# A two-layer decoder trunk on one core: tensors laid out on the host, no transposes, GpSimd silent in the recurrent part, another order of blocks

## The chip, the cores and the metric

The kernel runs on one core of a Trainium2 chip. A core has five engines that run their own instruction queues in order: TensorE (PE, matrix multiplies into PSUM; its weight loads are listed as PEld), VectorE (DVE), ScalarE (ACT), GpSimd (POOL) and SyncE (SP, which here only issues DMA transfers). They work on SBUF, an on-chip memory of 128 partitions, and wait for each other through semaphores. The metric is the device time of one execution in microseconds.

## The reference, cut to what matters

There are 1024 tokens of 1024 channels, and two layers. Layer 0 mixes tokens by a gated linear recurrence (RG-LRU), layer 1 by stick-breaking attention; each is followed by a dense SwiGLU network of width 2816, and a last RMS norm ends it.

```python
def rms_norm(x, g):
    return x * lax.rsqrt(jnp.mean(x * x, axis=-1, keepdims=True) + 1e-6) * g

def rg_lru_block(x, ...):
    u = x @ w_in + b_in                      # (1024 x 1024) @ (1024 x 2048)
    gate_branch, rec = u[..., :1024], u[..., 1024:]
    rec = causal_depthwise_conv(rec, conv_w, conv_b)          # 4 taps
    r, i = sigmoid(rec_blocks @ gate_w + gate_b)              # 4 diagonal blocks of 256
    log_a = -8 * r * softplus(-lam);  a = exp(log_a)
    h[t] = a[t] * h[t-1] + sqrt(-expm1(2 * log_a)) * (i * rec)[t]
    return (gelu(gate_branch) * h) @ w_out + b_out

for layer in range(2):
    h = h + mixer(rms_norm(h, mix_norm[layer]))
    h = h + swiglu_ffn(rms_norm(h, ffn_norm[layer]))
return rms_norm(h, final_norm)
```

All is fp32. The kernel keeps that precision by splitting each operand of a product into a high part (rounded to the fast fp32r type) and a low part (the difference), and by adding three products.

## The kernel before, in words

**Tiles.** Activations are kept with channels on the partitions: 8 channel tiles (ND) of 128, each as two halves (NH) of 512 tokens (NB). A product of a weight tile with a half is `mm3` (L141 to L143): three matmuls of 512 columns, high by high, high by low, low by high. A projection of one column of 128 output channels over both halves is 2 x 8 x 3 = 48 matmuls.

**First phase (L251 to L361).** x comes in token order, so TensorE transposes it (L301, 64 blocks of 128x128 against the identity). ScalarE writes the high part `xh` with the norm's gain (L304), VectorE the low part `xl` (L309), and a plain copy `hc` goes back to device memory as `hd` (16 stores), which is later loaded as the residual h. ScalarE takes the squares of the rows with a running sum (L314); from them come `rcol`, the 1/rms factors of the tokens, and `rbc`, the same factors spread over the partitions by small matmuls (L189). The norm's gains, biases and other vectors come in nine small loads as rows and are turned by one more transpose (L345). Beside this, the first two columns of the recurrent branch, A0 and A1, are projected. In this phase the order on every engine is written by hand.

**Recurrent block.** Blocks of work are named by a letter and an index, and their order is one string in the code:

```python
"A0 A1 B0 A2 G0 A3 Y0 B1 Y1 A4 G1 A5 B2 Y2 A6 G2 A7 B3 Y3 B4 Y4 G3 B5 Y5 B6 Y6"
```

A is a column of the recurrent branch: projection, scaling by `rbc` (`u`, L444), the four-tap convolution (`rec`, ScalarE L446 and three VectorE operations L448), and its split into `rh` (L450) and `rl` (L451). G is a pair of tiles: the two gates by matmuls over both tiles' `rh` and `rl`, then sigmoid, tanh, exp and square root on ScalarE (L472 to L480), seven elementwise operations and the recurrence itself on VectorE as one scan (L475 to L483). B is a column of the gate branch with its gelu (`gb`, L490, L491), Y the product of gelu and scan (L495). `last_tile` does B7 and splits the results for the output projection (`ob_ps`). By hand only TensorE's order is fixed here; a scheduler places the others' instructions by its own costs. The weights of a column are one load of 512 KB; ScalarE rounds the high part `whi` (L120), GpSimd subtracts for the low part `wlo` (L124), into a ring of three pairs of tiles. Products go to four PSUM tiles in turn (`ptile`).

**Middle.** The output projection, the first feed-forward network, attention (about 950 to 1500 us) and the second feed-forward network follow. The networks use a scheme of seven products in place of eight for each 2x2 arrangement of blocks; `ORDER` is the order of the seven, `Weights` loads and combines their weights, and `VISITS` lists the passes over the output. After each finished output tile `squares` adds its square to `acc`, on ScalarE (L211) and GpSimd (L212).

**End.** `finish` computes the last products of output tiles 0 and 4 (`last`, L1212 to L1225), the row statistics (`stats`), and in `turn` transposes the result back to token order (L1236, 64 blocks), scales it by `rcol` on ScalarE or VectorE (L1238, L1240) and stores it (L1241).

Of the kernel before, what the change touches and what calls it, by code (L numbers as in the profile page):

```python
# [29 lines left out]
V_MIX, V_FFN, V_FIN, V_BIN, V_CW, V_CB, V_GB, V_LAM, V_BO = 0, 16, 32, 40, 56, 88, 96, 112, 120  # L30


@with_exitstack
def trunk(
# [3 lines left out]
    mix_norm,  # L38
    ffn_norm,
    final_norm,  # L40
    lru_w_in,
    lru_b_in,
    lru_conv_w,
    lru_conv_b,
    lru_gate_w,
    lru_gate_b,
    lru_lambda,
    lru_w_out,
    lru_b_out,
# [5 lines left out]
    stage=None,  # L55
# [55 lines left out]
    def load_raw(src, shape):  # L111
        raw = rp.tile([P, D], F32, tag="raw", name="raw")
        view = raw if len(shape) == 1 else raw.rearrange("p (a b) -> p a b", a=shape[0])
        nc.sync.dma_start(view, src)
        return raw

    def split(raw, pool=None, tag="w", bufs=None, lo_eng=None, parts=1):
        pool = pool or wpool[0]
        hi = pool.tile([P, D], F32R, tag=tag, name="whi", bufs=bufs)
        nc.scalar.copy(hi, raw)  # L120
        lo = pool.tile([P, D], F32R, tag=tag, name="wlo", bufs=bufs)
        for i in range(parts):
            c = slice(i * D // parts, (i + 1) * D // parts)
            (lo_eng or nc.gpsimd).tensor_sub(lo[:, c], raw[:, c], f32(hi)[:, c])  # L124
        return hi, lo

    def cols(w, c0, n=P):
        return w[:, c0 : c0 + n].rearrange("(k p) c -> p k c", p=P)

    def load_cols(w, c0, **kw):  # L130
        hi, lo = split(load_raw(cols(w, c0), (ND,)), **kw)
        k3 = lambda t: t.rearrange("p (k c) -> p k c", k=ND)
        return k3(hi), k3(lo)

    def load_rows(w, r0, **kw):
        hi, lo = split(load_raw(w[r0 : r0 + P, :].rearrange("p (a b) -> p a b", a=1), (1,)), **kw)
        k3 = lambda t: t.rearrange("p (k c) -> p k c", k=ND)
        return k3(hi), k3(lo)
# [14 lines left out]
    class Mix:  # L153
# [8 lines left out]
        def load(self, i):  # L162
            self.raw[i] = load_raw(cols(self.src, self.order[i] * P), (ND,))
# [21 lines left out]
    def broadcast_r(ps_pool, tag, n):  # L185
        ps = ps_pool.tile([P, NB], F32, tag=tag, name="rb_ps")
        for i in range(4):
# [7 lines left out]
            )  # L195
        nc.vector.tensor_copy(rbc[n], ps)

    def stats(acc, ps_pool, tag, n, i0=0, i1=4):
        ps = ps_pool.tile([P, NB], F32, tag=tag, name="st_ps")
        for i in range(i0, i1):  # L200
# [28 lines left out]
    def open_h(nm):  # L229
# [3 lines left out]
        for j in range(ND // 2):  # L233
            for d in (j, j + ND // 2):
                for n in range(NH):
                    nc.sync.dma_start(h[d][n], hd[d][n])
# [4 lines left out]
    w_in, gw = lru_w_in[0], lru_gate_w[0]  # L241
# [8 lines left out]

    with ExitStack() as st, tc.manual_schedule(engines={E.PE, E.Activation, E.DVE, E.Pool, E.SP}):  # L251
        sp = st.enter_context(tc.tile_pool(name="sp", bufs=1))
        sps = st.enter_context(tc.tile_pool(name="sps", bufs=4, space=PSUM))
        vraw = sp.tile([P, P], F32, name="vraw")
        vmix = sp.tile([P, P], F32, name="vmix")
        g0 = sp.tile([P, ND], F32, name="g0")
        nc.scalar.dma_start(vmix[0:ND, :], mix_norm[0:1].rearrange("a (b c) -> (a b) c", c=P))
        xt = [sp.tile([P, 4, D], F32, name=f"xt{n}") for n in range(NH)]
        aw = []

        def load_x(n, g):
            cs = slice(g * 2 * P, (g + 1) * 2 * P)
            nc.sync.dma_start(
                xt[n][:, :, cs], x[0, n * NB : (n + 1) * NB, cs].rearrange("(i p) c -> p i c", p=P)
            )

        for g in range(3):
            load_x(0, g)
        aw.append(load_raw(cols(w_in, D), (ND,)))
        load_x(0, 3)  # L270
        aw.append(load_raw(cols(w_in, D + P), (ND,)))
        load_x(1, 0)
        load_x(1, 1)
        for base, src in (
            (V_MIX, mix_norm.rearrange("a (b c) -> (a b) c", c=P)),
            (V_FFN, ffn_norm.rearrange("a (b c) -> (a b) c", c=P)),
            (V_FIN, final_norm.rearrange("(b c) -> b c", c=P)),
            (V_BIN, lru_b_in.rearrange("a (b c) -> (a b) c", c=P)),
            (V_CW, lru_conv_w.rearrange("a k (b c) -> (a k b) c", c=P)),
            (V_CB, lru_conv_b.rearrange("a (b c) -> (a b) c", c=P)),  # L280
            (V_GB, lru_gate_b.rearrange("a g (b c) -> (a g b) c", c=P)),
            (V_LAM, lru_lambda.rearrange("a (b c) -> (a b) c", c=P)),
            (V_BO, lru_b_out.rearrange("a (b c) -> (a b) c", c=P)),
        ):
            nc.sync.dma_start(vraw[base : base + src.shape[0], :], src)
        load_x(1, 2)
        load_x(1, 3)
        ssum = sp.tile([P, NT], F32, name="ssum")
        ms = sp.tile([P, NT], F32, name="ms0")
        junk = sp.tile([P, D], F32, name="junk")  # L290
        pst = lambda name: sps.tile([P, NB], F32, tag="tp", name=name)
        k3 = lambda t: t.rearrange("p (k c) -> p k c", k=ND)

        ps = pst("vps0")
        nc.tensor.transpose(ps[:, 0:ND], vmix[0:ND, :], ident[0:ND, 0:ND])
        nc.vector.tensor_copy(g0, ps[:, 0:ND])

        def group(n, d):
            ps = pst("tp")
            for i in range(4):  # L300
                nc.tensor.transpose(ps[:, i * P : (i + 1) * P], xt[n][:, i, d * P : (d + 1) * P], ident)  # L301
            hc = sp.tile([P, NB], F32, tag="hc", name="hc", bufs=8)
            g = g0[:, d : d + 1]
            nc.scalar.activation(xh[d][n], ps, AF.Copy, scale=g)  # L304
            if d % 4 == 3:
                nc.scalar.copy(hc, ps)
            else:
                nc.vector.tensor_copy(hc, ps)
            nc.vector.scalar_tensor_tensor(xl[d][n], ps, g, f32(xh[d][n]), op0=ALU.mult, op1=ALU.subtract)  # L309
            nc.sync.dma_start(hd[d][n], hc)  # L310

        def square_rows(n, i):
            b = 4 * n + i
            nc.scalar.activation(junk, xt[n][:, i, :], AF.Square, accum_out=ssum[:, b : b + 1])  # L314

        def row_factors(n):
            nn = slice(4 * n, 4 * n + 4)
            nc.vector.tensor_scalar(ms[:, nn], ssum[:, nn], 1.0 / D, EPS, op0=ALU.mult, op1=ALU.add)
            rstd(rcol[:, nn], ms[:, nn])

        def wsplit(i):
            hi, lo = split(aw[i])
            aw[i] = (k3(hi), k3(lo))

        pa = [psl[0].tile([P, S], F32, tag="a", name="a_ps") for _ in range(2)]
        for d in range(6):
            group(0, d)
        wsplit(0)
        for d in (6, 7):
            group(0, d)  # L330
        wsplit(1)
        for i in range(4):
            square_rows(0, i)
# [192 lines left out]

# [1074 lines left out]
```

## Time and profile before

| | us |
|---|---|
| time, median of 3 runs (2211.14 to 2213.21) | 2211.43 |
| span of the profiled execution | 2213.1 |
| its own time | 2213.21 |
| TensorE busy | 2174.9 |
| VectorE busy | 1728.4 |
| ScalarE busy | 1152.4 |
| GpSimd busy | 288.8 |

The profiled execution is the slowest of the three, 1.8 above the median. Times in rows of a timeline are microseconds from the start of the span: start, duration, engine, line, operation, output <- inputs, shapes, count, and in brackets how long the engine had been idle before and what released it. Rows of groups give the count, the total busy time, the mean of one in ns, and the idle time before. Matmuls are pipelined: a row of 0.39 us is followed by the next one's start 0.23 us later. The lines that carry the argument stand in the prediction.

### The profile page before, as it was taken

The page shows a single profiled execution, that of the slowest core. Times are in us where ns is not written, and L with a number is a line of the kernel's source. Part 1 is how long each engine was busy: PE and PEld are TensorE (multiplying, and loading weights), DVE is VectorE, ACT ScalarE, POOL GpSimd, SP SyncE. Part 2 cuts the span into 40 slices and gives each one's busy share as a digit, 9 for nine tenths or more (in the row PEclk, how much of TensorE's full clock was granted, in tenths as well). Part 3 has the DMA queues.
Part 4 walks back from the last instruction along what each step waited for, and adds up shares of the span by engine and source line. Part 5 has one row for each costly group of instructions (what it writes and reads, how often), then busy time and mean ns, then how long its engine had stood idle before and what let it go on. Part 6 is the DMA issues. An engine that isn't in the chain of part 4 may idle for free.

```text
span 2213.1 us, 28506 instructions
## 1 busy us (share of the span) xinstructions
PE 2174.9 (98%) x10120; PEld 1802.8 (81%) x10120; DVE 1728.4 (78%) x2383; ACT 1152.4 (52%) x2031; POOL 288.8 (13%) x379
## 2 busy tenths in 40 slices
PE   8999999999999999999999999989999999999998
PEld 6888888888888888878888887878888888888887
DVE  6887778677777887878888888876876777788876
ACT  5577444444444544656666666653533444454556
POOL 2222020000000000004333333331000000000002
PEclk9999999999999999999999999999999999999999
DMA  7111412334443864453333333532133444467442
GB/s 230 48 48 38 133 39 71 106 124 152 143 157 133 272 194 123 144 144 85 95 89 102 98 88 99 169 137 71 39 110 124 148 147 137 149 233 231 136 148 86
DMA packets 298703, 277.74 MB, mean 125 GB/s; under 512 B 16312, under 2 KB 215104, under 8 KB 298560
## 3 DMA queue, kind: packets, MB, share of 16 engines
q1 hardware_dynamic: 298544, 275.91, 40.0%
q8 instruction: 80, 1.31, 0.2%
q14 instruction: 63, 0.52, 0.1%
q10 hardware_dynamic: 16, 0.00, 0.0%
HBM read 175.71 MB, written 74.97 MB: 113 GB/s over the span
## 4 chain that ended last, share of the span: by engine, by line
PE 84%; DVE 8%; ACT 3%; DMA 2%; issue 1%; SPq 1%; DVEq 0%; ACTq 0%
PE p_ps L143 18%; PE p_ps L141 18%; PE p_ps L142 18%; PE ob_ps L141 2%; PE ob_ps L142 2%; PE ob_ps L143 2%; PE qk_ps L143 2%; PE qk_ps L141 2%; PE qk_ps L142 2%; PE a_ps L143 2%; PE a_ps L142 2%; PE a_ps L141 2%; PE wt_ps L1437 2%; DVE F L1425 2%; PE z_ps L1400 1%
## 5 line engine op out<-in xcount | busy, mean ns | idle before, releaser
L1426 POOL TENSOR_TENSOR w<-w,F 128x128 f32<-128x128 f32 (+1 forms) x192 | 185.2, 965 | 315.0 <-DVE F L1423 177.6
L143 PE MATMUL p_ps<-vh,wcl 128*128 128x512 f32 x524 | 204.2, 390 | 0.5 <-DVE wcl L682 0.5
L143 PE MATMUL p_ps<-vh,wbl 128*128 128x512 f32 x524 | 204.3, 390 | 0.3 <-DVE wbl L672 0.2
L143 PE MATMUL p_ps<-vh,wal 128*128 128x512 f32 x524 | 204.1, 389 | 0.1
L141 PE MATMUL p_ps<-vh,wbh 128*128 128x512 f32 x524 | 204.2, 390 | 0.0
L141 PE MATMUL p_ps<-vh,wch 128*128 128x512 f32 x524 | 204.1, 389 | 0.0
L142 PE MATMUL p_ps<-vl,wbh 128*128 128x512 f32 x524 | 203.9, 389 | 0.0
L142 PE MATMUL p_ps<-vl,wch 128*128 128x512 f32 x524 | 203.9, 389 | 0.0
L142 PE MATMUL p_ps<-vl,wah 128*128 128x512 f32 x524 | 203.9, 389 | 0.0
L141 PE MATMUL p_ps<-vh,wah 128*128 128x512 f32 x524 | 203.9, 389 | 0.0
L668 ACT CAST wbh<-sb 128x1024 fp32r<-128x1024 f32 (+2 forms) x69 | 69.6, 1009 | 193.6 <-DVE sb L652 193.6
L212 POOL TENSOR_TENSOR acc<-acc,rbc 128x512 f32<-128x512 f32 x30 | 40.5, 1349 | 773.3 <-ACT rbc L211 773.3
L1423 DVE TENSOR_TENSOR_SCAN F<-F,unit 128x128 f32<-128x128 f32 (+3 forms) x128 | 128.5, 1004 | 4.4 <-ACT F L1419 4.3
L1446 ACT CAST th<-wt_ps 128x512 fp32r<-128x512 f32 x192 | 93.3, 486 | 73.2 <-PE wt_ps L1437 71.2
L1447 DVE TENSOR_TENSOR tl<-wt_ps,th 128x512 fp32r<-128x512 f32 x192 | 104.9, 547 | 29.1 <-ACT th L1446 28.1
L141 PE MATMUL qk_ps<-vh,whi 128*128 128x512 f32 x264 | 118.4, 449 | 0.6 <-ACT vh L215 0.6
L143 PEld LDWEIGHTS p_ps<-vh,wbl 128*128 128x128 f32 x524 | 98.3, 188 | 22.4 <-DVE wbl L672 2.0
L143 PEld LDWEIGHTS p_ps<-vh,wcl 128*128 128x128 f32 x524 | 98.3, 188 | 22.0 <-DVE wcl L682 1.6
L143 PEld LDWEIGHTS p_ps<-vh,wal 128*128 128x128 f32 x524 | 98.3, 188 | 21.4 <-DVE wal L663 1.0
L142 PEld LDWEIGHTS p_ps<-vl,wch 128*128 128x128 f32 x524 | 98.4, 188 | 20.4
L141 PEld LDWEIGHTS p_ps<-vh,wbh 128*128 128x128 f32 x524 | 98.4, 188 | 20.4 <-ACT ta L1053 0.2
L142 PEld LDWEIGHTS p_ps<-vl,wah 128*128 128x128 f32 x524 | 98.3, 188 | 20.4
(400 smaller groups left out, 5837.7 us busy)
## 6 DMA issues: line engine op xcount, KB each, us to landing
raw<-in_ffn_w_in SPq DMA_DIRECT2D x88, 512.0 KB, 3.9
vl<-pd SPq DMA_DIRECT2D x128, 256.0 KB, 3.7
pd<-U SPq DMA_DIRECT2D x90, 256.0 KB, 2.3
raw<-in_ffn_w_out SPq DMA_DIRECT2D x56, 256.0 KB, 3.8
raw<-in_attn_w_qkv SPq DMA_DIRECT2D x24, 512.0 KB, 3.9
raw<-in_lru_w_in SPq DMA_DIRECT2D x16, 512.0 KB, 4.1
acc<-pd SPq DMA_DIRECT2D x28, 256.0 KB, 2.6
pph<-rbc SPq DMA_DIRECT2D x28, 256.0 KB, 2.5
```

Of the source, the lines that this page charges most:

```text
L141: nc.tensor.matmul(ps, lhsT=wh, rhs=mh, start=first, stop=False, **kw)
L142: nc.tensor.matmul(ps, lhsT=wh, rhs=ml, start=False, stop=False, **kw)
L143: nc.tensor.matmul(ps, lhsT=wl, rhs=mh, start=False, stop=last, **kw)
L212: (eng or nc.gpsimd).tensor_add(acc[n], acc[n], sq)
L668: nc.scalar.copy(self.full(self.wb), self.full(self.sb))
L1400: nc.tensor.matmul(ps[:, 0 : c1 - c0], lhsT=lhsT, rhs=KL[q][hx][:, c0:c1], start=False, stop=True)
L1423: nc.vector.tensor_tensor_scan(rev, rev, unit[:, NB - n :][:, ::-1], first, op0=ALU.mult, op1=ALU.add)
L1425: nc.vector.tensor_tensor_scan(rev, rev, rev, first, op0=ALU.mult, op1=ALU.bypass)
L1426: nc.gpsimd.tensor_mul(wt, wt, F[:, 1 : n + 1])
L1437: nc.tensor.transpose(tp[:, c : c + P], W[q, hx, j, kb // 4][:, (kb % 4) * P : (kb % 4 + 1) * P], ident)
L1446: nc.scalar.copy(th[:, q0:], tp[:, q0:])
L1447: nc.vector.tensor_sub(tl[:, q0:], tp[:, q0:], f32(th)[:, q0:])
```

## The change

- The host lays out x as [channel tile, half, 128, 512], the weights as tiles whose partition lines are contiguous, and the vectors as one `table` that is one load, on ScalarE's queue. The result is stored as [channel tile, half, 128, 512] and put in order by the host. All transposes on TensorE are gone, `hc` and `hd`'s first stores too: h is loaded from x.
- The first phase projects four columns, `FIRST` = A0, A1, B0, A2, from `lru_first`, which holds their weights by k. For half 0 the four are interleaved over k, each k as soon as its x tile and weights are there; then half 1 column by column. Squares of x are taken tile by tile on ScalarE, added on VectorE, and summed over partitions by small matmuls (`column_stats`). All four PSUM tiles are taken in this phase.
- In the recurrent block the low parts of weights are subtracted on VectorE rather than GpSimd. The `+ 1.0` on `a` goes from VectorE to ScalarE. The order of the blocks is another.
- In the second network the squares' adds go from GpSimd to VectorE, the last visit's products come in another order, of which 3 and 6 are handed to `finish`, the last weights have tiles of their own (`we`), and the square root's table is loaded early.
- `finish` spreads the factors over the partitions (`factor`) and multiplies each output tile (`give`), on VectorE or, for some tiles, on GpSimd, before storing it; the last stores alternate between the queues of SyncE and ScalarE.

The core of the diff:

```diff
+FIRST = (ND, ND + 1, 0, ND + 2)
...
-            (lo_eng or nc.gpsimd).tensor_sub(lo[:, c], raw[:, c], f32(hi)[:, c])
+            (lo_eng or nc.vector).tensor_sub(lo[:, c], raw[:, c], f32(hi)[:, c])
...
+        for k in range(ND):
+            nc.sync.dma_start(xr[k][0], x[k, 0])
+            nc.sync.dma_start(fr[k].rearrange("p (t c) -> p t c", t=4), lru_first[k])
+        for k in range(ND):
+            nc.sync.dma_start(xr[k][1], x[k, 1])
...
+        bank = half(pa[FIRST[3]], 1)
+        for k in range(ND):
+            nc.scalar.copy(fh[k], fr[k])
+            x_hi(k, 0)
+            x_square(k, 0)
+            nc.vector.tensor_sub(fl[k], fr[k], f32(fh[k]))
+            x_lo(k, 0)
+            if k:
+                x_add(k - 1, 0)
+            for t, j in enumerate(FIRST):
+                c = slice(t * P, (t + 1) * P)
+                mm3(half(pa[j], 0), fh[k][:, c], fl[k][:, c], xh[k][0], xl[k][0], k == 0, k == ND - 1)
+        x_add(ND - 1, 0)
+        for k in range(ND):
+            x_hi(k, 1)
+            x_lo(k, 1)
+        for k in range(3):
+            x_square(k, 1)
...
+        def second(i, ks):
+            for k in ks:
+                c = slice(i * P, (i + 1) * P)
+                mm3(half(pa[FIRST[i]], 1), fh[k][:, c], fl[k][:, c], xh[k][1], xl[k][1], k == 0, k == ND - 1)
+
+        def spread_to(n):
+            spread(bank, n)
+            nc.vector.tensor_copy(rbc[n], bank)
+
+        column_stats(sacc[0], bank, 0)
...
+        second(0, range(4))
+        spread_to(0)
...
+        second(0, range(4, ND))
+        second(1, range(4))
+        column_stats(sacc[1], bank, 1)
+        second(1, range(4, ND))
+        second(2, range(2))
+        spread_to(1)
+        second(2, range(2, ND))
+        second(3, range(ND))
...
-                V.tensor_scalar_add(a, a, 1.0)
+                nc.scalar.activation(a, a, AF.Identity, bias=1.0)
...
-            for what in "A0 A1 B0 A2 G0 A3 Y0 B1 Y1 A4 G1 A5 B2 Y2 A6 G2 A7 B3 Y3 B4 Y4 G3 B5 Y5 B6 Y6".split():
+            for what in "A0 A1 B0 A2 B1 G0 A3 Y0 Y1 A4 B2 G1 A5 Y2 A6 B3 Y3 G2 A7 B4 Y4 G3 B5 Y5 B6 Y6".split():
...
-                    squares(h, d, n, rbc, acc, first=n not in begun_sq)
+                    squares(h, d, n, rbc, acc, V, first=n not in begun_sq)
...
+                rest = [lambda: tail(3, range(3)), lambda js: tail(6, js)]
+                for k, i in enumerate((0, 1, 2, 4, 5) if last_two else ORDER):
...
+        def factor(n, i0, i1):
+            cs = slice(i0 * P, i1 * P)
+            spread(half(ob, n), n, i0, i1)
+            nc.scalar.copy(half(rs, n)[:, cs], half(ob, n)[:, cs])
+
+        def give(n, i0, i1, ds, slow=(), queues=(nc.sync,)):
+            cs = slice(i0 * P, i1 * P)
+            for k, d in enumerate(ds):
+                t = h[d][n][:, cs]
+                if d in slow:
+                    nc.gpsimd.tensor_mul(t, t, half(rs, n)[:, cs])
                 else:
+                    nc.vector.tensor_mul(t, t, half(ob, n)[:, cs])
+                queues[k % len(queues)].dma_start(out[d, n][:, cs], t)
...
+        for x in range(2):
+            last(x, *first)
+        third()
+        sixth(range(0, 1))
+        stats(acc[0], pp, "p", 0)
+        sixth(range(1, 3))
+        last(0, *mid)
+        factor(*first)
+        give(*first, (1, 2, 3, 5), (3,))
+        last(1, *mid)
+        give(*first, (6, 7, 0, 4), (7,))
+        last(0, *end)
+        stats(acc[1], pp, "p", 1, 0, 2)
+        last(1, *end, lambda: factor(*mid), lambda: give(*mid, (1, 3), (3,)))
+        give(*mid, (2, 5))
+        stats(acc[1], pp, "p", 1, 2, 4)
+        give(*mid, (6, 7, 0, 4), (7, 4))
+        factor(*end)
+        give(*end, (1, 2, 3, 5, 6, 0, 7, 4), (3, 7), (nc.sync, nc.scalar))
```

More of the change, by code (lines that the diff above doesn't have):

```diff
@@ L54, in trunk @@
     out,
-    stage=None,
 ):
@@ L162, in load @@
         def load(self, i):
-            self.raw[i] = load_raw(cols(self.src, self.order[i] * P), (ND,))
+            self.raw[i] = load_raw(self.src[self.order[i]])
         def proc(self, i):
@@ L183, in rstd, with spread @@
         nc.vector.tensor_mul(dst, sq, t)
-    def broadcast_r(ps_pool, tag, n):
-        ps = ps_pool.tile([P, NB], F32, tag=tag, name="rb_ps")
-        for i in range(4):
+    def spread(ps, n, i0=0, i1=4):
+        for i in range(i0, i1):
             b = 4 * n + i
@@ L195, in broadcast_r @@
             )
+    def broadcast_r(ps_pool, tag, n):
+        ps = ps_pool.tile([P, NB], F32, tag=tag, name="rb_ps")
+        spread(ps, n)
         nc.vector.tensor_copy(rbc[n], ps)
@@ L286, in trunk @@
[L286 to L325, printed above, removed]
@@ L1191, in mix_out_ffn_in @@
                 nxt = ahead
-                if kind == "v" and not final:
+                if kind == "v" and final:
+                    if x == 2:
+                        open_end()
+                elif kind == "v":
                     if x == 2:
```

311 lines of the change are left out of this document (125 added, 186 removed).

## The prediction

> **What bounds the kernel now.** I read the page first (busy shares, the chain that ended last), then windows of the stages that the change touches, then timelines at the start, between the last two gate stages and at the tail.
>
> ```profile
> PE 2174.9 (98%) x10120; PEld 1802.8 (81%) x10120; DVE 1728.4 (78%) x2383; ACT 1152.4 (52%) x2031; POOL 288.8 (13%) x379
> PE 84%; DVE 8%; ACT 3%; DMA 2%; issue 1%; SPq 1%; DVEq 0%; ACTq 0%
> ```
>
> TensorE is busy for 98% of the span of 2213.1 us, so the change pays only where it removes work of TensorE, its idle time or its cold clock. The windows say where these are (window, length, busy time of PE, PEld, DVE, ACT, POOL, granted clock, DMA share, GB/s):
>
> ```profile
> 0.00:50.00 50.00, 39.25 (x198) 32.28 (x199) 30.91 (x77) 29.52 (x46) 13.19 (x12) 1.00 0.75 244
> 100.00:150.00 50.00, 50.00 (x223) 41.39 (x222) 44.35 (x35) 30.32 (x28) 14.44 (x5) 1.00 0.17 49
> 154.30:198.80 44.50, 44.50 (x197) 36.60 (x195) 38.65 (x30) 29.66 (x27) 11.86 (x4) 1.00 0.17 48
> 2186.30:2207.30 21.00, 17.59 (x141) 16.41 (x139) 14.02 (x38) 13.26 (x24) 0.22 (x1) 1.00 0.40 149
> ```
>
> The start holds 10.75 us of idle TensorE, and the tail 3.4. In the recurrent block TensorE never rests, and VectorE comes next with 44.35 of 50.
>
> **Start.** The first transposes, warm ones later, the projections, and the end of the recurrent stage:
>
> ```profile
> 4.52 4.55 PE L301 MATMUL tp<-ident,xt 128*128 128x128 f32 x20 [1.18 <-DMA xt<-in_x]
> 19.12 1.03 PE L301 MATMUL tp<-ident,xt 128*128 128x128 f32 x8
> L304 ACT ACTIVATE xh<-tp,g 128x512 fp32r<-128x512 f32 x16 | 10.3, 686 | 2.2 <-PE tp L301 2.2
> L309 DVE SCALAR_TENSOR_TENSOR xl<-tp,g,xh 128x512 fp32r<-128x512 f32 x16 | 11.5, 739 | 0.0
> L451 DVE TENSOR_TENSOR rl<-rec,rh 128x1024 fp32r<-128x1024 f32 x8 | 9.8, 1219 | 0.0
> L450 ACT CAST rh<-rec 128x1024 fp32r<-128x1024 f32 x8 | 8.4, 1050 | 26.1 <-DVE rec L448 26.1
> 41.77 1.16 PE rb_ps L189 x8
> 240.26 0.39 PE L141 MATMUL a_ps<-xh,whi 128*128 128x512 f32 x1
> 241.62 0.39 PE L141 MATMUL ob_ps<-xh,whi 128*128 128x512 f32 x1
> ```
>
> Between the last two rows lie six matmuls: 1.36 / 6 = 0.227 us each. The stage has 20 blocks of 48 matmuls (16 projected columns, 4 gate blocks). The changed kernel projects four of them at the start; the other 16 are 768 matmuls, 174.3 us. The kernel before has that much left at 241.6 - 174.3 = 67.3. When does the changed one?
> Its first x tile and first weight slice are 512 KB together, as one x piece was before, so they land near 4.5 us; two ScalarE operations of the 686 ns kind follow, and the first matmul starts at 5.8. Per k TensorE has 12 x 0.227 = 2.7 us; VectorE 3 x 0.7 = 2.1; ScalarE about 2.0; the transfer of 512 KB at the window's 244 GB/s 2.1. So TensorE sets the pace: 96 x 0.227 = 21.8 us. The 20 first transposes took 4.55 us, warm ones 1.03 / 8 = 0.129 each, so a cold start costs 4.55 - 20 x 0.129 = 2.0 us; it was spent on transposes beside waiting and now falls on real matmuls. Half 0 ends at 5.8 + 21.8 + 2.0 = 29.6. Half 1 is 21.8 more; the two spreads are the 1.16 of the rb_ps row, the 8 small statistics matmuls about as much. One wait is new: on VectorE's queue three splits of later weights (L116, 1.22 each) stand ahead of the statistics of half 0, so the row factors come near 34.8 while TensorE wants to spread them at 33.0; I take 1.0 of that 1.8. End of the first phase: 29.6 + 21.8 + 1.2 + 1.2 + 1.0 = 54.8; gain 12.5 us (bounds 9 to 16: all waits doubled, or none and a warm clock). The nine vector loads, the 16 write-backs of h and their copies were off TensorE's path, and SP's queue only gets shorter: nothing.
> The Trainium skill ("TensorE: Matmul & The Clock Gate", Part 1) has the first 3.4 us of activity at half clock, in a window that runs freely; it speaks against the change, which puts projections there. Half of 3.4 is 1.7 us by that estimate, so the rule makes the gain 12.8 and not 12.5.
>
> **Recurrent block.** The stretch between gate stages G2 and G3, with its split operations on GpSimd:
>
> ```profile
> 154.30 0.39 PE L141 MATMUL g_ps<-rh,whi 128*128 128x512 f32 x1
> 162.42 1.28 DVE L448 SCALAR_TENSOR_TENSOR rec<-u,vc,rec 128x1024 f32<-128x1024 f32 x1
> 164.40 1.23 DVE L475 TENSOR_TENSOR gs<-gs,rec 128x1024 f32<-128x1024 f32 x1 [0.69 <-ACT gs L473]
> 167.80 1.22 DVE L477 SCALAR_TENSOR_TENSOR ga<-ga,gt 128x1024 f32<-128x1024 f32 x1 [1.04 <-ACT ga L476]
> 169.06 1.23 DVE L478 SCALAR_TENSOR_TENSOR ga<-ga,gt 128x1024 f32<-128x1024 f32 x1
> 170.32 1.23 DVE L479 SCALAR_TENSOR_TENSOR gt<-ga 128x1024 f32<-128x1024 f32 x1
> 172.59 0.69 DVE L481 TENSOR_SCALAR ga<-ga 128x1024 f32<-128x1024 f32 x1
> 174.64 1.23 DVE L482 TENSOR_TENSOR gs<-gs,gt 128x1024 f32<-128x1024 f32 x1 [1.36 <-ACT gt L480]
> 175.90 2.29 DVE L483 TENSOR_TENSOR_SCAN y<-ga,gs 128x1024 f32<-128x1024 f32 x1
> 178.09 3.46 POOL L124 TENSOR_TENSOR wlo<-raw,whi 128x1024 fp32r<-128x1024 f32 x1 [18.57 <-ACT whi L120]
> 179.34 3.29 DVE L478 SCALAR_TENSOR_TENSOR ga<-ga,gt 128x1024 f32<-128x1024 f32 x1
> 183.16 2.82 DVE L479 SCALAR_TENSOR_TENSOR gt<-ga 128x1024 f32<-128x1024 f32 x1
> 189.23 2.56 POOL L124 TENSOR_TENSOR wlo<-raw,whi 128x1024 fp32r<-128x1024 f32 x1 [4.34 <-ACT whi L120]
> 189.46 4.48 DVE L483 TENSOR_TENSOR_SCAN y<-ga,gs 128x1024 f32<-128x1024 f32 x1
> 198.84 0.50 PE L142 MATMUL g_ps<-rl,whi 128*128 128x512 f32 x1
> ```
>
> Three VectorE operations that met a split of GpSimd took 3.29, 2.82 and 4.48 where their likes took 1.23, 1.23 and 2.29: 5.8 us that go with GpSimd. In return VectorE gets two or three splits of 1.22 per stretch and gives one kind of 0.69 (L481) to ScalarE, which has 20 of 50 us free.
> The Trainium skill ("SBUF — State Buffer", Who interferes with whom) calls the shared port an exclusive lock: a VectorE instruction with two SBUF inputs and a GpSimd one that reads SBUF shut each other out for the whole instruction. The three rows agree; by it the splits cost VectorE more on GpSimd (about 2 us each) than the 1.22 on its own queue.
> What counts is when rl of tile 7 is ready, the last input of G3 (the 198.84 row; before, it came just in time, with A7, B3 and B4 behind G2). The new order moves B3 ahead of G2: from G2's start only G2, A7 and B4 are left, 3 x 48 x 0.227 = 32.7, and rl is needed 0.9 later (fifth matmul), at 33.6. VectorE's queue: it meets G2's first result 164.40 - 154.30 = 10.1 after its start; from there to rl stand, in the new order, 13 operations of 1.22, two scans (4.6), two u and two gb halves of 0.69 (2.8) and three L448 of 1.28 (3.8): 27.1, and the waits for ScalarE of 1.04 and 1.36 stay. 10.1 + 27.1 + 2.4 = 39.6: **G3 stalls 6.0 us** (bounds 0, where rl is pulled ahead to the end of A7 at 21.8 + 9; and 11, with the 5.85 us idle that VectorE has in the window row). G1 and G2 keep four blocks of distance, 43.6, against 38.6 of VectorE's work: no stall up to 5 us idle.
> **G0 stalls 2.6 us:** the order puts B1 ahead of G0, and ScalarE's queue has the high part of A4's weights (a cast like rh, 1.05), which needs the ring slot that B1's last matmul frees, ahead of rh of tile 1 (1.05); rl (1.22) follows; 0.7 is covered by G0's first three matmuls, which need tile 0 alone (0 to 4). Behind that cast on ScalarE wait rh, gb and rec; behind rl on VectorE gb.
>
> **Attention and FFN.** Weights come in whole lines of 4 KB instead of 512 B. The waits that a faster transfer could touch:
>
> ```profile
> PE z_ps L1399 <- DMA kh<-qh__12230: 1.8, 1, 1.8
> PE z_ps L1400 <- DMA kl<-ql__9211: 0.6, 1, 0.6
> ```
>
> They wait for copies of q and k inside the kernel, not for weights, which come long before: 0 (-3 to +2). The ten squares' adds that leave GpSimd for VectorE (0.69 each) lie in FFN visits under a full TensorE: 0, up to +1.5 if one of them is ahead of a split that is due.
>
> **Tail.** The last product's first matmul, the table load, adds of 256 and 512 columns, a small step, and the last scaling and issues:
>
> ```profile
> 2183.49 0.39 PE L141 MATMUL o_ps<-vh,wah 128*128 128x512 f32 x1
> 2184.30 1.08 DVE L701 TENSOR_TENSOR wrl<-raw,wrh 128x512 fp32r<-128x512 f32 x1
> 2191.13 0.42 DVE L1222 TENSOR_TENSOR hh<-o_ps,hh 128x256 f32<-128x256 f32 x1
> 2190.52 0.69 DVE L1224 TENSOR_TENSOR acc<-acc,rbc 128x512 f32<-128x512 f32 x1 [0.70 <-ACT rbc L1223]
> 2193.80 1.28 ACT L178 ACT_TABLE_LOAD   x1
> 2202.16 0.16 DVE L180 TENSOR_TENSOR rs_t<-rs_s 128x2 f32<-128x2 f32 x1
> 2205.82 1.41 DVE L1240 TENSOR_SCALAR U<-e_ps,rcol 128x512 f32<-128x512 f32 x2
> 2205.11 4.11 SPq L1241 DMA_DIRECT2D out<-U  x5
> ```
>
> Products 3 and 6 (18 matmuls, 4.1 us) move behind the finish's first pieces, so I count from 2179.4 in both: before, the last scaling ends 27.8 later. After, TensorE has 64 transposes less, but VectorE sets the pace: 15 operations of 0.69, 19 of 0.42, 18 small of 0.16 are 21.2; with the 7.0 us idle of the window row less the table load 1.28, and 1 us to the first, 27.9. The last stores go out on two queues of four instead of five on one (0.82 each): 0.6 less. Sum -0.5 (-3.5, VectorE's idle halved; +2.5, if its adds meet GpSimd's seven multiplications as L701 did at 1.08).
>
> **Sum.** -12.5 + 2.6 + 6.0 + 0 - 0.5 = -4.4: 2208.7 in the profiled frame. The median of the runs, 2211.43, is 1.7 below that frame's 2213.1, so 2207.0.
>
> **Rivals.** (1) The stalls do not come: VectorE keeps ahead, ScalarE's cast finds a free slot. For it, VectorE loses 5.8 us of disturbance per stretch; against it, the queue orders above. -13.0: 2198.4. (2) Opposite side: VectorE becomes the bound of every stretch. Each us of idle beyond 5 in 43.6 is a stall at G1, at G2 and on top of G3's; the window row shows 5.85. At 8 us idle (each of the stretch's waits on ScalarE 1 us longer, as it now also does L481): 3 + 3 + 3 more, +4.6: 2216.0. It decides from 7.9 us on. For it, 44.35 of 50; against it, the 5.8 that go. (3) The start saves less, because its transfers come late or the statistics hold TensorE: gain 9, and 0.9 is left: 2210.5.
>
> **Numbers.** The runs tell a difference of about 0.2%, 4.4 us: 2207.0 and 2215.9 are the bounds. Forecast 0.44 (2203 to 2211; half of it below 2207), rival 1 0.30, rival 2 0.14, rival 3 0.12. Faster 0.22 + 0.30 + 0.02 = 0.54; slower 0.14 and 0.04 of a worse tail = 0.18; same 0.28. Range 2197 to 2217.
>
> **What would show it.** The first phase ends near 55 us (wrong if after 58); TensorE idles about 2.6 before G0 and 6 before G3, with rl named; VectorE's L478 and L479 all at 1.23; the first matmul of the output projection near 238; the last scaling 28 us after the end of product 5. If TensorE is idle at G1 and G2 too, rival 2 holds; if nowhere, rival 1.

## The result and the profile after

The changed kernel takes 2218.49 us (median of 12 runs, 2215.52 to 2223.05) against 2212.34 for the kernel before (median of 12, 2210.53 to 2215.7): a ratio of 1.0027, 95% interval 1.0018 to 1.0035. It is slower by about 6 us; 2207 was forecast, the range ended at 2217. The profiled execution is the slowest of the twelve (2223.05 us); its span of 2221.3 us stands against 2213.1 of the kernel before, so the traces differ by 8.2 us where the medians differ by 6.

The page of the changed kernel, shares of the span and the chain by engine:

```profile
PE 2172.0 (98%) x10022; PEld 1798.9 (81%) x10022; DVE 1722.2 (78%) x2418; ACT 1147.8 (52%) x2030; POOL 224.2 (10%) x356
PE 80%; DVE 11%; ACT 5%; issue 2%; DMA 1%; SPq 0%; DVEq 0%; ACTq 0%
```

TensorE is busy for 3 us less and the span is 8 us longer: TensorE waits more, for VectorE and ScalarE, whose shares of the chain grew. What it waited for, over the whole span and without the rows of attention (total us, times, longest):

```profile
PE g_ps L125 <- ACT rh L406: 7.3, 2, 6.2
PE a_ps L125 <- ACT xh L262: 5.9, 1, 5.9
PE st_ps L191 <- DVE acc L1193: 3.5, 2, 1.9
PE ob L172 <- DVE rcol L167: 2.2, 1, 2.2
PE ob L172 <- DVE hh L1208: 2.1, 1, 2.1
PE p_ps L125 <- ACT ta L1002: 1.9, 3, 0.8
PE p_ps L125 <- ACT tb L1002: 1.5, 2, 0.8
PE g_ps L126 <- DVE rl L407: 1.2, 2, 0.8
```

The first and the last row are the recurrent block, the second is the start of the kernel, the other five are the end, but for 0.4 us of the row of `ta`, which lie in the first network. The starts of the stages on TensorE, from its timeline:

```profile
5.88 0.80 PE L125 MATMUL a_ps<-xh,fh 128*128 128x512 f32 x1 [5.88 <-ACT xh L262]
67.00 0.39 PE L125 MATMUL g_ps<-rh,whi 128*128 128x512 f32 x1
189.20 0.39 PE L125 MATMUL g_ps<-rh,whi 128*128 128x512 f32 x1
196.21 0.79 PE L125 MATMUL g_ps<-rh,whi 128*128 128x512 f32 x1 [6.16 <-ACT rh L406]
197.47 0.79 PE L126 MATMUL g_ps<-rl,whi 128*128 128x512 f32 x1 [0.47 <-DVE rl L407]
242.66 0.39 PE L125 MATMUL ob_ps<-xh,whi 128*128 128x512 f32 x1
```

G0 starts at 67.0 with five columns done; the kernel before was there with five blocks done at 67.3 + 10.9 = 78.2. So the start gained 11 us. By the output projection, at 242.66 against 241.62, all of it is gone again. Two windows of the block's last part, and the last 32 us up to the last multiplication (columns as in the prediction):

```profile
189.20:196.20 7.00, 0.84 (x4) 0.38 (x2) 6.93 (x8) 2.10 (x4) 0.00 (x0) 0.74 0.26 75
196.20:210.02 13.82, 13.35 (x45) 10.43 (x46) 6.36 (x7) 10.99 (x10) 0.00 (x0) 0.76 0.13 39
2184.65:2216.85 32.20, 21.16 (x123) 18.17 (x121) 20.94 (x54) 12.72 (x25) 6.21 (x7) 0.89 0.29 103
```

In the first, VectorE works for 6.93 of 7.00 us while TensorE waits; in the second G3 runs at a mean clock of 0.76. The same stretch of the end before, from the finish's first matmul to the last scaling, stands in this window of the kernel before:

```profile
2183.49:2207.25 23.76, 20.40 (x153) 18.75 (x151) 15.70 (x40) 15.34 (x27) 2.69 (x2) 1.00 0.36 132
```

The account of the 8.2 us between the traces: start -11.1, G0 +2.5 (80.40 - 67.00 - 10.88, the next block's start against its own), G3 +9.9 (210.02 - 189.20 - 10.88), against 0.3 that the kernel before lost at its own G3; attention +2.1; the last visits of the second network +2.1 of waits; the finish +2.9. Without attention's 2.1, which are no effect of the change (see below), 6 us are left, as between the medians.

### The profile page after: what moved, and what is told of

The parts are those of the page before. It is cut to its first block, busy times and chain, and to the rows that moved or that the text cites. A ratio compares the mean times of both kernels' runs of the same rounds, so it can differ in the third digit from the quotient of the medians.

```text
span 2221.3 us, 28188 instructions
## 1 busy us (share of the span) xinstructions
PE 2172.0 (98%) x10022; PEld 1798.9 (81%) x10022; DVE 1722.2 (78%) x2418; ACT 1147.8 (52%) x2030; POOL 224.2 (10%) x356
## 4 chain that ended last, share of the span: by engine, by line
PE 80%; DVE 11%; ACT 5%; issue 2%; DMA 1%; SPq 0%; DVEq 0%; ACTq 0%
PE p_ps L127 18%; PE p_ps L125 18%; PE p_ps L126 17%; PE qk_ps L127 3%; PE qk_ps L125 3%; PE qk_ps L126 3%; PE ob_ps L125 2%; PE ob_ps L126 2%; PE ob_ps L127 2%; PE wt_ps L1404 2%; DVE F L1392 2%; PE a_ps L125 1%; PE a_ps L126 1%; PE a_ps L127 1%; PE z_ps L1367 1%
## 5 line engine op out<-in xcount | busy, mean ns | idle before, releaser
L125 PEld LDWEIGHTS p_ps<-vh,wch 128*128 128x128 f32 x524 | 98.4, 188 | 21.5 <-ACT tb L1002 1.3
```

Source lines behind the costliest of these rows:

```text
L125: nc.tensor.matmul(ps, lhsT=wh, rhs=mh, start=first, stop=False, **kw)
```

## The experiments

All ratios are to the kernel before, which ran on the same chip beside each. Its medians there are 2211.7 to 2212.8 us, so a difference between two kernels that ran on different chips is good to about 1 us. B5 ahead of G3 became the base of most later kernels.

**e1: block B5 ahead of G3.** In the changed kernel's order string:

```diff
-... B3 Y3 G2 A7 B4 Y4 G3 B5 Y5 B6 Y6
+... B3 Y3 G2 A7 B4 Y4 B5 G3 Y5 B6 Y6
```

> One edit to the changed kernel: block B5 is moved ahead of G3, so that four blocks (G2, A7, B4, B5: 43.5 us) instead of three (32.7) lie between the starts of G2 and G3; two blocks (B6, B7) are left behind G3. Distance theory (rl of tile 7 comes 39.6 us after G2's start, whatever TensorE does meanwhile; the idle time then costs half clock on top): the idle 6.6 us at G3 and the slow matmuls behind it, 9.9 us in the profiled run of the changed kernel, are gone, the output projection begins near 232.7 instead of 242.7, and the time falls by 8 to 10 us against the changed kernel, to about 2209. Rival, VectorE as the bound of the whole stage: the wait only moves, to the output projection, whose operands then come as late as before; gain 0 to 3 us.

2210.32 us, ratio 0.9993 (0.9984 to 1.0001): 8.2 below the changed kernel. The wait at G3 is gone, and the output projection comes at

```profile
231.86 0.39 PE L125 MATMUL ob_ps<-xh,whi 128*128 128x512 f32 x1
```

10.8 us earlier; 1.1 us of small waits follow in it (the largest is `ob_ps` for `gb`, 0.9). VectorE is not the bound of the stage: the wait doesn't move elsewhere, it was the distance of three blocks.

**e2: the order of the kernel before.** The changed kernel with the order string of before.

> One edit to the changed kernel: the block order of the kernel before, with the four columns still projected up front, so G0 comes right behind the first phase, B1 behind G0, and each of G1, G2, G3 has four blocks ahead of it. Distance theory: no wait at G3; a wait at G0, since rl of tile 1 has only the first phase's last column and a half to hide behind (0 to 8 us); G1 to G3 free; output projection at 233 to 240, time 3 to 9 us below the changed kernel. Rival (VectorE is the bound): waits at G1 and G2 too, output projection not before 242.

2218.00 us, 1.0030 (1.0019 to 1.0042): no gain, and a miss, for 3 to 9 us less were expected. G1 to G3 run free, as the distance theory has it, but its expected price at G0 was too low. G0's waits in TensorE's timeline:

```profile
62.18 0.80 PE L125 MATMUL g_ps<-rh,whi 128*128 128x512 f32 x1 [5.92 <-ACT rh L406]
63.58 0.79 PE L126 MATMUL g_ps<-rl,whi 128*128 128x512 f32 x1 [0.61 <-DVE rl L407]
65.92 0.79 PE L125 MATMUL g_ps<-rh,whi 128*128 128x512 f32 x1 [1.12 <-ACT rh L406]
67.47 0.80 PE L126 MATMUL g_ps<-rl,whi 128*128 128x512 f32 x1 [0.76 <-DVE rl L407]
```

8.4 us of waits and matmuls of 0.79: without B1 ahead of it G0 costs as much as G3 did. So B1 ahead of G0 is worth its place; what was missing is a block ahead of G3.

**e3: low parts on GpSimd again.** In the changed kernel, for the columns and gates of the recurrent block:

```diff
-        hi, lo = split(load_raw(src))
+        hi, lo = split(load_raw(src), lo_eng=nc.gpsimd)
...
-            hi, lo = split(raw)
+            hi, lo = split(raw, lo_eng=nc.gpsimd)
```

> One edit to the changed kernel: the low parts of the recurrent block's weights are subtracted on GpSimd again, as before. Port theory (each split on GpSimd holds up a VectorE operation for about 2 us, on VectorE it costs 1.22): rl of tile 7 comes later by about 3 us, G3's wait grows from 6.6 to 8 to 11 us, time 2 to 5 us above the changed kernel. Rival (VectorE's length of work is what counts, and GpSimd took work off it): the wait shrinks by 2 to 4 us and the time falls by as much.

2225.39 us, 1.0064 (1.0051 to 1.0076): 6.9 slower than the changed kernel, more than expected. VectorE's scan and convolution, first in the changed kernel, then in this one:

```profile
L404 DVE SCALAR_TENSOR_TENSOR rec<-u,vc,rec 128x1024 f32<-128x1024 f32 x21 | 26.9, 1280 | 0.1
L439 DVE TENSOR_TENSOR_SCAN y<-ga,gs 128x1024 f32<-128x1024 f32 x8 | 18.3, 2285 | 0.2
```

```profile
L404 DVE SCALAR_TENSOR_TENSOR rec<-u,vc,rec 128x1024 f32<-128x1024 f32 x21 | 31.1, 1481 | 0.4
L439 DVE TENSOR_TENSOR_SCAN y<-ga,gs 128x1024 f32<-128x1024 f32 x8 | 24.9, 3108 | 0.0
```

These two kinds alone take 10.8 us more. The Trainium skill's rule in "SBUF — State Buffer" (Who interferes with whom) agrees with these rows. VectorE's sum of work does not grow, for the 13 splits of 1.22 us that left its queue are 15.9 us. What grows is the way to the gates: between G2 and G3 one scan takes 4.49 us where its like takes 2.27, VectorE also waits longer for ScalarE, and TensorE's wait for `rh` at G3 is 8.3 us in place of 6.2. So the port theory has the direction right and its size too low; that the stretched operations count because they stand in this chain is read from the trace, not tested alone.

**e8: low parts on VectorE in the kernel before**, the same edit the other way round in `split` (`nc.vector` for `nc.gpsimd`).

> One edit to the kernel before: the low parts of the recurrent block's weights are subtracted on VectorE instead of GpSimd, in the first phase too; the order of the blocks stays. Since TensorE is busy in every window of the block there, nothing can be gained: time within 2 us of the kernel before. VectorE's work in the stretch from G2 to G3 falls (three operations lose 5.8 us, two splits of 1.22 come): rl of tile 7 no longer waits. Rival (VectorE's load decides): G3 waits by 1 to 4 us, the time grows by as much.

2212.61 us, 1.0002 (0.9993 to 1.0011): no difference. With four blocks of distance TensorE does not see what VectorE saves; silence of GpSimd is worth 0 there, and 7 us in the tighter order of e3.

**e11: TensorE kept busy through G3's wait.** In the changed kernel, in its own order:

```diff
                     ps = ptile("g_ps")
+                    for _ in range(28 if (b, i, g) == (3, 0, 0) else 0):
+                        nc.tensor.matmul(half(ps, 0), lhsT=xh[0][0][:, :P], rhs=xh[0][0], start=True, stop=True)
```

> The changed kernel in its own order, with 28 extra matmuls of 512 columns ahead of G3's first one, on operands that are there already; their result is overwritten. They fill 6.4 us, about the wait for rl of tile 7, which stays. Clock theory (the idle TensorE falls to half clock, and 6.5 us of matmuls behind the wait then run at half speed, 3.3 us lost): G3 runs at 0.227 us per matmul, the output projection begins near 239.4 instead of 242.7, time 2 to 4 us below the changed kernel (2218.5). Rival (the slow matmuls have another cause, such as late operands): no difference, or slower.

2214.32 us, 1.0009 (1.0000 to 1.0018): 4.2 below the changed kernel (3.5, if each is taken against the kernel before beside it), with 28 matmuls more. G3 itself, once they are through:

```profile
194.59 0.39 PE L125 MATMUL g_ps<-rh,whi 128*128 128x512 f32 x1
195.27 0.45 PE L125 MATMUL g_ps<-rh,whi 128*128 128x512 f32 x1
196.49 0.50 PE L126 MATMUL g_ps<-rl,whi 128*128 128x512 f32 x1 [0.77 <-DVE rl L407]
```

rl is no earlier, but the matmuls run at full clock, and the output projection starts at 239.25. So of the 9.9 us at G3 some 6.6 are the wait, and 3.3 the half clock that the wait brings.

**e4: products 3 and 6 back in their visit.** In the changed kernel:

```diff
-                for k, i in enumerate((0, 1, 2, 4, 5) if last_two else ORDER):
+                for k, i in enumerate(ORDER):
...
-                rest = [lambda: tail(3, range(3)), lambda js: tail(6, js)]
+                rest = [lambda: None, lambda js: None]
```

> One edit to the changed kernel: in the last but one visit of the second network products 3 and 6 stand in their old places and order again, and the finish does nothing in their stead; all else of the new end stays. Theory that the new product order costs (waits for the copies ta and tb of 0.75, 0.67 and 0.84 us ahead of the finish, and 0.67 in it): 2 to 3 us of these go, but the finish loses 4.1 us of matmuls that covered the statistics of the first half, so that wait returns; net -2 to +2 us against the changed kernel. Rival (the waits come from the adds on VectorE and the early table load, not from the order): +2 to +4 us.

2219.75 us, 1.0033 (1.0021 to 1.0045): the same as the changed kernel within the intervals, as expected. Of the three waits for copies ahead of the finish only the first is left (0.8 us), the one behind the early table load. In its trace the visits take 2.1 us less beside the 4.1 of the moved matmuls, the finish as much more: without the cover TensorE waits for the statistics.

**e5: the whole end of the kernel before**, on the start and block order of e1: order of products, squares' adds on GpSimd, `finish` with its transposes, result in token order.

> The changed kernel's start and recurrent block (with B5 ahead of G3), and the whole end of the kernel before: its order of products, the squares' adds on GpSimd, no early table load, the transposes and the result in token order. Theory that the new end costs about 5 us against the old one (from the first matmul of the finish to the last store 36.6 us, of which 4.1 are the two products moved there, against 29.6; and 2.1 us of waits ahead of it): time near 2203 to 2205, 5 to 7 us below the changed kernel with B5 ahead of G3 (2210.3). Rival, as predicted at first, that the two ends take the same time and the rest was lost to the clock in attention: 2209 to 2211.

2203.83 us, 0.9959 (0.9946 to 0.9971): as expected. It is 6.5 below e1, which differs in the end alone (7.3, if each is taken against the kernel before beside it), and 9 below the kernel before. Over the last 100 us TensorE's waits are three, the same as in the kernel before:

```profile
PE e_ps L1202 <- ACT y L1204: 0.7, 1, 0.7
PE e_ps L1202 <- ACT U L1204: 0.7, 1, 0.7
PE p_ps L127 <- DVE wbl L619: 0.2, 1, 0.2
```

**e10: e5 with the root's table loaded earlier**, behind the first two of the last products.

```diff
             for x in range(2):
                 last(x, *piece)
+            if piece is first:
+                nc.scalar.sqrt(early[:, 0:1], ones)
```

> The kernel with the new start and the old end (2203.8), with one edit: the square root's table is loaded behind the first two of the last products, where ScalarE has 1.3 us free, and not inside the statistics. Theory (the table load of 1.28 us stands in the chain from the statistics to the first scaling, and all later pieces follow that chain on VectorE): time 0.5 to 1.5 us lower. Rival (the later pieces wait for TensorE and for the stores): no difference.

2203.26 us, 0.9960 (0.9947 to 0.9972): 0.6 less, inside the expectation, but the intervals of e5 and e10 cover each other; the two theories are not told apart. It is the fastest of all kernels run here, by that margin.

**e6: a finish without quarters.** On e1, products 3 and 6 in their visit, the square root's table loaded inside the finish, three of eight tiles of each half on GpSimd, and:

```diff
-        first, mid, end = (0, 0, 4), (1, 0, 2), (1, 2, 4)
+        first, second = (0, 0, 4), (1, 0, 4)
...
+        last(0, *second)
+        stats(acc[0], pp, "p", 0)
+        last(1, *second, lambda: factor(*first), lambda: give(*first, (1, 3), (3,)))
+        stats(acc[1], pp, "p", 1)
+        give(*first, (2, 5, 7, 6, 0, 4), (5, 7))
+        factor(*second)
+        give(*second, (1, 2, 3, 6, 5, 0, 7, 4), (3, 5, 7), (nc.sync, nc.scalar))
```

> The changed kernel with B5 ahead of G3; products 3 and 6 back in their visit, the square root's table loaded in the finish, and a finish without the split of the second half into two quarters: the four last products of 512 columns run one behind the other on TensorE, each half gets its statistics once, and GpSimd takes three of eight tiles of each half. Theory (the new finish is long because TensorE's last products wait in the queue behind statistics and spreads, which wait for VectorE, which works off multiplications in between): TensorE's products end 8.2 us after the first of them, the last multiplication comes near 18 us and the end near 23 us after it, against 29.6 before; time 2196 to 2202. Rival (the finish is bound by VectorE's sum of work, or by the stores): the end comes 28 us or more after it, and the time is 2203 or more.

2207.93 us, 0.9978 (0.9969 to 0.9987): 2.4 better than e1, and a miss: 2196 to 2202 was expected. TensorE's waits in its end:

```profile
PE ob L172 <- DVE hh L1207: 3.9, 1, 3.9
PE st_ps L191 <- DVE acc L1192: 2.6, 1, 2.6
```

The second spread writes one half of the shared tile `ob` and waits for VectorE's multiplications out of the other half.

**e9: e6 with factor tiles of their own.** Each spread goes to two new PSUM tiles, one for VectorE, one for ScalarE's copy:

```diff
-            spread(half(ob, n), n, i0, i1)
-            nc.scalar.copy(half(rs, n)[:, cs], half(ob, n)[:, cs])
+            fac[n, i0] = pp.tile([P, NB], F32, tag="p", name="f_ps")
+            copied = pp.tile([P, NB], F32, tag="p", name="f_ps")
+            spread(fac[n, i0], n, i0, i1)
+            spread(copied, n, i0, i1)
+            nc.scalar.copy(half(rs, n)[:, cs], copied[:, cs])
```

> The kernel with the unsplit finish (2207.9), with one edit: each spread of the row factors goes to two PSUM tiles of its own, one that VectorE multiplies from and one that ScalarE copies. In the unsplit finish TensorE waited 3.9 us for VectorE's multiplications of the first half before it could spread the second half's factors into the other half of one shared tile, though those factors were ready 2.4 us earlier; and VectorE waited for ScalarE's copy. Theory (the shared tile is what makes the finish long): the second spread starts about 2.4 us earlier and the multiplications behind it 2.5 to 3.5 us earlier, time 2204 to 2206. Rival (the sum of VectorE's work, or the half clock of small matmuls): within 1 us of 2207.9.

2205.82 us, 0.9970 (0.9958 to 0.9982), 2.1 less: within the expectation, and still 2 behind the old end.

**e12: own factor tiles in the finish of the changed kernel** (on e1, one tile per spread).

> The changed kernel with B5 ahead of G3 (2210.3), with one edit in its finish: each spread of the row factors has a PSUM tile of its own instead of a part of one shared tile. Theory of the shared tile: the last spread no longer waits for the multiplications of the quarter before (0.7 us behind its factors), nor the one before it; 0.5 to 1.5 us less. Rival (the chain of each quarter's statistics, two quarters one behind the other, sets the end): no difference.

2210.18 us, 0.9994 (0.9986 to 1.0003): no difference to e1. In this finish the shared tile is not what sets the end.

**e7: VectorE alone multiplies** (on e1, `slow` empty everywhere).

> The changed kernel with B5 ahead of G3, and VectorE alone multiplies in the finish (GpSimd none). Port theory (GpSimd's multiplications hold up the adds of squares: 0.71 us in place of 0.42): VectorE gets 7 operations of 0.37 to 0.63 us more and loses a stretch of 0.3 to 0.7: time 0 to 3 us above the kernel with GpSimd (2210.3). Rival (the port costs more than that): below it.

2212.41 us, 0.9998 (0.9989 to 1.0007): 2.1 above e1, as expected for seven more operations on VectorE, though the intervals overlap. GpSimd's hold on VectorE's adds doesn't outweigh its help here.

**e13: multiplications late.** On e12, VectorE's multiplications of the first half behind the adds of all last products and the last statistics:

```diff
-        give(*first, (1, 2, 3, 5), (3,))
         last(1, *mid)
-        give(*first, (6, 7, 0, 4), (7,))
         last(0, *end)
         stats(acc[1], pp, "p", 1, 0, 2)
-        last(1, *end, lambda: factor(*mid), lambda: give(*mid, (1, 3), (3,)))
+        last(1, *end, lambda: factor(*mid), lambda: give(*first, (1, 3), (3,)))
...
+        give(*first, (2, 5), ())
+        give(*first, (6, 7, 0, 4), (7,))
```

> The kernel with a PSUM tile of its own for each spread of factors (2210.2), with one edit: VectorE's multiplications of the first half come behind the adds and squares' adds of all four last products, and behind the last statistics, instead of ahead of them. Queue theory (six multiplications, 3.8 us, stand in VectorE's queue ahead of the adds of the last quarter, and the last statistics wait for those): the last statistics come 2 to 4 us earlier; part of it is given back where the multiplications now stand behind them; time 1 to 3 us below 2210.2. Rival (VectorE's sum of work and its waits for ScalarE are what fill the finish, in whatever order): within 1 us of 2210.2, or above it.

2209.74 us, 0.9990 (0.9981 to 0.9999): 0.4 below e12, no difference. The last statistics and the last multiplications on VectorE, in e12 and then here:

```profile
2197.39 0.16 DVE L193 TENSOR_SCALAR ms<-st_ps 128x2 f32<-128x2 f32 x1 [0.44 <-PE st_ps L191]
2200.56 2.08 DVE L1211 TENSOR_TENSOR hh<-hh,f_ps 128x256 f32<-128x256 f32 x6 [1.12 <-ACT held L1202]
```

```profile
2193.03 0.16 DVE L193 TENSOR_SCALAR ms<-st_ps 128x2 f32<-128x2 f32 x1 [0.70 <-PE st_ps L191]
2194.33 6.72 DVE L1211 TENSOR_TENSOR hh<-hh,f_ps 128x512 f32<-128x512 f32 x16
```

The finish began at 2171.1 in e12 and at 2170.2 here, so the last statistics did come 3.5 us earlier, and then sixteen multiplications of 6.72 us together stand behind them. VectorE no longer waits for ScalarE's copy of the factors either, and still the finish is as long, from its first matmul to the end of the span 35.9 us against 35.7. The step that the queue theory names came true and its gain did not: the order only moves VectorE's work about.

**e14: e13 with two tiles per spread**, so that VectorE needs no tile that ScalarE reads.

> The kernel with late multiplications, with one edit: the factors are spread twice, to a tile that VectorE multiplies from and one that ScalarE copies for GpSimd, so that VectorE no longer waits for the copy (0.4 to 0.6 us ahead of each of three groups). Theory: 0.5 to 1.5 us less than with one tile. Rival (the extra matmuls at half clock cost what the wait saves): no difference.

2211.77 us, 1.0000 (0.9991 to 1.0009): no gain; a miss. It is 2.0 above e13, and its finish is 1.6 us longer in the trace.

## Why the prediction was wrong

Between the -4.4 of the forecast and the 6 us measured lie some 10.5 us. The traces put 5.5 of them at the end, 3.6 at G3 and 1.4 at the start.

**Start: right in kind, 1.4 us too high.** The first matmul was put at 5.8 and came at 5.88; the first phase was to end at 54.8 and G0, one block later, starts at 67.00, so it ended at 56.1. The wait of 1.0 us for the row factors did not come. In its place the statistics and spreads took 1.9 and 2.1 us, not 1.2 each: the `rb_ps` row of 1.16 us, which the prediction took for two spreads, is one. And the cold start cost about 1 us more than 2.0, for half 0 ended at 30.6 in place of 29.6: matmuls follow each other at 0.43 us here (8.11 and 8.54 in the two rows below).

```profile
8.11 0.63 PE L126 MATMUL a_ps<-xl,fh 128*128 128x512 f32 x1
8.54 0.63 PE L127 MATMUL a_ps<-xh,fl 128*128 128x512 f32 x1
L172 PE MATMUL a_ps<-ident,rcol 128*128 128x128 f32 x16 | 2.1, 274 | 0.0
L191 PE MATMUL a_ps<-ones,sacc 128*128 128x1 f32 x16 | 1.9, 239 | 0.0
```

**G0: right.** 2.6 predicted, 2.5 in the trace. The rows name `rh` and `rl`, and ScalarE does cast A4's weights (at 66.98) just ahead of `rh` (at 67.93).

```profile
69.02 0.50 PE L125 MATMUL g_ps<-rh,whi 128*128 128x512 f32 x1 [1.18 <-ACT rh L406]
70.28 0.49 PE L126 MATMUL g_ps<-rl,whi 128*128 128x512 f32 x1 [0.76 <-DVE rl L407]
```

**G1 and G2: right.** No wait; the rival that VectorE bounds every stretch is out, though the time fell on that rival's side.

**G3: the mechanism right, the term mis-sized.** The wait of 6.6 us answers to the 6.0, and `rl` of tile 7 came 40.9 us after G2's start, against 39.6 in the sum. Most of the wait is for `rh` (6.2), which is cast from the same late convolution. What the term left out is the clock: the prediction priced the half clock at the start, where its rows showed it, and not behind a wait of 6 us in the middle of the kernel. That is 3.3 us in the trace, and e11 gives 4.2 in time. e1 shows that the whole of it hangs on the three blocks of distance.

**GpSimd: right in direction.** With GpSimd silent the operations of L478 and L479 take 1.22 us each (here L434 and L435), as predicted. Its price depends on the order: 7 us in the tight one (e3), nothing in that of the kernel before (e8). The "about 2 us each" of the prediction's three rows is not the mean: in e3 the scans and convolutions lose 10.8 us to 13 splits. So VectorE's sum of work is not the reason; in e3's trace the slow operations stand in the chain that leads to G3.

**The end: the step that failed.** "Sum -0.5" became about +5 in the traces (2.1 ahead of the finish, 2.9 in it), 6.5 in time (e5 against e1). Two parts of that step were wrong. The visit ahead of the finish was costed at nothing; but with products 3 and 6 gone, product 4 follows 2 and 5 follows 4 with nothing between them that uses another PSUM bank, and TensorE waits for ScalarE's copies each time, beside one wait behind the early table load:

```profile
2176.30 0.50 PE L125 MATMUL p_ps<-vh,wbh 128*128 128x512 f32 x1 [0.75 <-ACT ta L1002]
2179.30 0.50 PE L125 MATMUL p_ps<-vh,wbh 128*128 128x512 f32 x1 [0.67 <-ACT tb L1002]
2182.47 0.50 PE L125 MATMUL p_ps<-vh,wch 128*128 128x512 f32 x1 [0.84 <-ACT tb L1002]
```

And in the finish VectorE's work was counted rightly (21.2; 20.94 in its window), but its idle time was taken over from the old finish, 7.0 less the table load. It is 32.20 - 20.94 = 11.3. VectorE's longest waits in the two finishes, the changed one first:

```profile
DVE hh L1208 <- ACT held L1199: 3.2, 3, 1.7
DVE acc L1193 <- ACT rbc L1191: 2.8, 5, 0.7
DVE acc L202 <- ACT rbc L201: 1.4, 2, 0.7
```

```profile
DVE acc L1224 <- ACT rbc L1223: 3.4, 6, 0.8
DVE rs_s L179 <- ACT rs_s L178: 2.1, 3, 1.6
```

The waits for the copies of the factors (`held`, 3.2) had no term in the sum at all, and those for squares grew from 3.4 to 4.2, since products 3 and 6 now bring theirs into the finish. For TensorE's products VectorE waits no longer than before (2.8 against 3.0). TensorE's last products stand in its queue behind statistics and spreads that wait for VectorE (3.5, 2.2 and 2.1 in the rows of the result). The old finish gives half of its scalings to ScalarE (VectorE 15.70 busy, ScalarE 15.34 in 23.76); the new one leaves ScalarE at 12.72 of 32.20. e13 shows that neither another order of the multiplications nor the end of VectorE's waits for the copy helps; e12 and e14 that a tile for each spread and a second spread gain nothing; e7 that taking GpSimd's share away tends to make it worse. That the sum of VectorE's work with the chains of statistics between sets the end is what these leave; no run here moved multiplications to ScalarE, so it is not shown directly.

**Attention: predicted 0, +2.1 in the traces.** The code is unchanged but for the weights' layout. The stretch from the last matmul of the first network to the output projection:

```profile
963.80:1482.90 519.10, 502.32 (x2641) 419.74 (x2640) 440.59 (x614) 329.06 (x810) 190.68 (x322) 0.99 0.38 105
```

```profile
964.80:1486.10 521.30, 505.35 (x2642) 422.74 (x2642) 438.26 (x614) 329.17 (x810) 190.52 (x322) 0.98 0.37 104
```

```profile
956.80:1472.10 515.30, 500.88 (x2642) 418.56 (x2641) 439.88 (x614) 329.32 (x810) 192.16 (x322) 0.99 0.38 105
```

These are the kernel before, the changed one and e10, which has the changed one's attention. The last two differ by 6 us, so the +2.1 is no effect of the change; the granted clock differs between them. Thirteen kernels of the experiments, e10 among them, have the changed kernel's attention. In their traces the time from attention's first matmul to the second network's statistics is 622.9 to 626.7 us; it is 629.1 in the changed kernel's trace and 627.0 in that of the kernel before.

Undone one by one, G3 (-8.2, e1) and the end (-6.5, e5) bring 2218.5 to 2203.8; what is left of the change makes the kernel 9 us faster than before. In the trace the start's 11.1 less G0's 2.5 account for that; no run here takes the new start alone.

## What to carry to other kernels

In a block order, count for each consumer how many blocks stand between it and the stage that feeds it, and compare with the length of the other engine's queue from the one to the other: one block too few cost 6.6 us here, and moving one block gave them back. Price a wait of some microseconds on TensorE with the half clock behind it: it added half of the wait again. When a finish is rewritten, take the new finish's idle times from its own chain of waits; the old one's idle time does not carry over, and a layout that saves TensorE its transposes can move the scaling from an engine with room to the one that has none (here read from the busy times, not tested).

## What the runs showed of the hardware that was not expected

After the wait of 6.6 us at G3, TensorE's matmuls follow each other at 0.43 us for 6.5 us more before they return to 0.227; 28 matmuls without use in that gap made the kernel 4.2 us faster. And the same attention code took 515.3, 519.1 and 521.3 us in three profiled executions, with a mean granted clock of 0.99, 0.99 and 0.98: this stretch varies from execution to execution by more than most of the terms of this study. Why it does is not shown here.
